# Sums of weight quarters in a seven-product matmul: from accumulating DMAs to VectorE and GpSimd

## The chip, the cores and the metric

The kernel runs on one core of a Trainium2 chip. The metric is device time in microseconds. The kernel before took 545.22, 550.09 and 551.16 us in three runs, a median of 550.09 us. The profiled execution that all rows below come from took 547.97 us, of which the recorded span is 546.2 us.

A core has five engines with instruction streams of their own, each worked off in order: TensorE (PE in the profile, with its weight loads as PEld), VectorE (DVE), ScalarE (ACT), GpSimd (POOL) and SyncE (SP, which here only issues DMAs). Data wait in on-chip memory (SBUF); TensorE writes its results to PSUM; 16 DMA engines move data from and to DRAM. A semaphore tells one engine that another, or a DMA, is done.

## The reference

Two residual layers over x of 512 rows and 1024 columns, in float32:

```
layer 0: h = rms_norm(x);  y = h @ W_in          # one projection, its columns are:
         [FoX q,k,v | forget logits | MoBA q,k,v | gate]
         FoX attention (8 heads, decay bias)  ||  MoBA attention (8 heads, rotary, top-3 blocks)
         x = x + (concat(heads) * silu(gate)) @ W_out
layer 1: h = rms_norm(x);  y = h @ W_in1          # GLU value | GLU gate | gate
         GLU -> causal depthwise conv (31 taps) -> layer norm -> swish -> * silu(gate)
         x = x + y @ W_out1
```

The change is in layer 0's input projection.

## The kernel before

**Products.** A float32 matmul is done as three matmuls: both sides are split into a high part of type float32r and the rest, and hi·hi, hi·lo and lo·hi are added in PSUM. `parts_of` makes such a split: an ACT copy for the high part (L412), then a DVE subtraction for the rest (L413). A split result is called an operand here.

**Seven products.** Ten of the column chunks of 256 columns of layer 0's projection are taken in five pairs (`PAIRS`, n = 0 to 4). The two chunks of a pair, 1024 x 512 values, are cut into four quarters: "11" and "12" are the upper 512 rows of the first and the second chunk, "21" and "22" the lower ones. A quarter lies in SBUF as 128 x 1024 float32, 512 KB. A Strassen-like scheme multiplies a pair with 7 products in place of 8. `product` (L608) is 24 matmuls of 128x256. The left sides (sums of quarters of h) are made once, ahead; the right sides are, with b for the quarters of the pair:

| product | 1 | 7 | 2 | 5 | 6 | 3 | 4 |
|---|---|---|---|---|---|---|---|
| right side | b11 | b12+b22 | b21 | b11+b12 | b11+b12+b22 | b22 | b11+b12+b21+b22 |

Each right side is one operand: one L412 and one L413, 35 in all. This text writes (n,m) for product m of pair n and op(n,m) for its operand. The list `PRODS` orders them as 7, 2, 5, 6 of pair n, then 1 of pair n+1, then 3 and 4 of pair n. `make_to` makes operands two products ahead (`AHEAD`), into three buffers.

**Staging.** Two tiles of SBUF (`stage`, tag "wst") hold four quarters, that is one pair. A quarter of the next pair is fetched by SP into the place of a quarter that is done with. The first four pairs use L559; the last pair's columns are split, so its fetches are the lines L561, L563 and L564.

**Sums in the kernel before.** They are made by DMA: GpSimd issues a transfer from DRAM with `accum_op=add`, which adds a quarter to one that is staged. Four stand in each pair: b22 onto "12" when "12" has been fetched; then "12" onto "11" once op(n,1) is made; "11" onto "12" once op(n,7) is made; "21" onto "12" once op(n,6) is made. All sums but that of op(n,5) end in the place "12", which op(n,7), op(n,6) and op(n,4) are read from. A DMA of this kind waits on the DVE subtraction that read its place last.

**What runs beside it.** The products are interleaved with attention work (`advance`, `PACE`): q and k are scaled and split (L757 and L758, L766 to L768), logits are formed (L777, L779), masked with their row maximum (L789, DVE), exponentiated (L790, ACT), transposed (L793, L803) and multiplied by v (L874). After each product ACT and DVE combine results (L627, L642 to L646: the running sums of the scheme), and rows are normalized (L483 to L501 on ACT, DVE and GpSimd, the rotary steps L505 to L511 on GpSimd). The framework's scheduler fixes each engine's order when the program is built. Layer 1 comes after, from about 300 us; there GpSimd and DVE share the convolution (L1042, L1052).

Of the kernel before, what the change touches and what calls it, by code (L numbers as in the profile page):

```python
# [14 lines left out]
ALU = mybir.AluOpType  # L15
# [14 lines left out]
WC = 256  # L30
# [63 lines left out]
PAIRS = ((2, 5), (3, 4), (7, 8), (10, 11), (9, 6))  # L94
# [4 lines left out]
def tile_kernel(ctx: ExitStack, tc: tile.TileContext, x, xt, w, small0, small1, l1_norm, out):  # L99
# [15 lines left out]
    V, A, G, T, SY = nc.vector, nc.scalar, nc.gpsimd, nc.tensor, nc.sync  # L115
# [52 lines left out]
    def w_cols(i, k, c, m):  # L168

        off, n = wsrc[i]  # L170
        return bass.AP(tensor=w.tensor, offset=w.offset + off + k * n + c,
                       ap=[[KC * n, P], [n, KC // 2 if m != NH else KC], [1, m]])

    def w_ap(off, n, k, m):
        return bass.AP(tensor=w.tensor, offset=w.offset + off + k * n,
                       ap=[[KC * n, P], [1, m * n]])
# [58 lines left out]
    HK = KC // 2  # L235
    HT = S // 2

    def operand(x):

        x = x.rearrange("p (j k n) -> p j k n", j=2, k=HK)  # L240
        return x[:, 0], x[:, 1]
# [34 lines left out]
    wsrc = []  # L276
# [112 lines left out]
    for t in range(NT):  # L389
        ts = slice(t * P, (t + 1) * P)  # L390
        for h in range(2):
# [3 lines left out]
                            op=ALU.mult)  # L395
# [14 lines left out]
    def parts_of(x, dst, eng=V):  # L410
        hi, lo = dst
        A.activation(hi, x, AF.Copy)  # L412
        eng.tensor_tensor(lo, x, hi.bitcast(F32), op=ALU.subtract)  # L413
# [100 lines left out]
    def qk_chunk(i, key, rope_i):  # L514
# [12 lines left out]
        if i:  # L527
# [8 lines left out]

    place = {"11": 0, "12": 1, "21": 2, "22": 3}

    NEXT = {"11": "21", "12": "11", "21": "22", "22": "12"}
    places = []  # L540


    OPERANDS = {1: ("11", "12"), 7: ("12", "11"), 2: ("21", None), 5: ("11", None),
                6: ("12", "21"), 3: ("22", None), 4: ("12", None)}

    PRODS = [(n + a, m) for n in range(-1, len(PAIRS)) for a, m in
             ((0, 7), (0, 2), (0, 5), (0, 6), (1, 1), (0, 3), (0, 4)) if 0 <= n + a < len(PAIRS)]
# [2 lines left out]
    def quarter(n, q):  # L550
        j = places[n][q]
        return stage[j // 2][:, j % 2 * HK * WC:(j % 2 + 1) * HK * WC].rearrange(
            "p (k n) -> p k n", k=HK)

    def from_b(queue, n, q, d, **kw):

        i, k = PAIRS[n][int(q[1]) - 1], (int(q[0]) - 1) * HK
        if n < FPAIR:
            queue.dma_start(d.rearrange("p k n -> p (k n)"), w_ap(*wsrc[i], k, HK), **kw)  # L559
        elif q[1] == "1":  # L560
            queue.dma_start(d, w_cols(i, k, 0, WC), **kw)  # L561
        else:
            queue.dma_start(d[:, :, 4:], w_cols(i, k, 0, WC - 4), **kw)  # L563
            queue.dma_start(d[:, :, :4], w_cols(PAIRS[n][0], k, WC, 4), **kw)  # L564

    def fetch_quarter(n, q):
        if n >= len(PAIRS):
            return
        if n == len(places):
            places.append({x: places[-1][y] for x, y in NEXT.items()} if n else  # L570
                          {"11": 0, "12": 1, "21": 2, "22": 3})
        from_b(SY, n, q, quarter(n, q))
        if q == "12":
            from_b(G, n, "22", quarter(n, q), accum_op=ALU.add)

    def fetch_first():
        for _ in range(2):
            stage.append(main.tile([P, KC * WPAD], F32, tag="wst", name="stage", bufs=2))
        for q in ("11", "12", "21", "22"):
            fetch_quarter(0, q)  # L580
# [4 lines left out]
    def make_to(g):  # L585

        while made[0] <= min(g, len(PRODS) - 1):
            n, m = PRODS[made[0]]
            q, more = OPERANDS[m]
            tag = slots[made[0] % 3]  # L590
            made[0] += 1
            ops[n, m] = operand(main.tile([P, KC * WPAD], F32R, tag=tag, name="op",
                                          bufs=2 if tag == "whi" else 1)[:, :2 * HK * WC])
            parts_of(quarter(n, q), ops[n, m])
            if more:
                from_b(G, n, more, quarter(n, q), accum_op=ALU.add)
            for x, y in NEXT.items():
                if y == q and m in (2, 5, 3, 4):
                    fetch_quarter(n + 1, x)

    def product(po, a, b, new):
# [9 lines left out]
    def pairs_of_chunks(jobs):  # L611
# [7 lines left out]
        for g, (n, m) in enumerate(PRODS):  # L619
            job = jobs[n]  # L620
            make_to(g + AHEAD)
            b = ops.pop((n, m))
            if m == 1:
# [277 lines left out]
    def dense():  # L901
        with tc.issue_after(hpart.ins):
            split(1)
        fetch_first()
        sums()
        yield from qk_chunk(0, ("moba", "q", 0), 0)
        make_to(1)
        yield from qk_chunk(1, ("moba", "k", 0), 1)
        last_sum()
        for j, _ in enumerate(pairs_of_chunks((Values("moba"), QK("moba", 1, True), QK("fox", 0, False),  # L910
                                               QK("fox", 1, False), Values("fox")))):
            if j == len(PRODS) - 3:
                fetch(12)
                fetch(13)
            yield
        split(12)
        spread_rinv()
        for c in range(4):
            fetch(14 + c)
            split(13 + c)  # L920
            yield from gate_chunk(12 + c, c)
# [29 lines left out]
    for k in KORD:  # L951
# [3 lines left out]
        eng = G if k in GLO else V  # L955
# [200 lines left out]
    for c in range(1, 4):  # L1156
        i = 20 + 2 * c
# [91 lines left out]
    n = max(len(v6), len(v7))  # L1249
# [38 lines left out]
    with tc.manual_schedule(engines=engs):  # L1288
# [19 lines left out]
        for p in range(4):  # L1308
            k = 2 * p
# [153 lines left out]
```

## Time and profile before

| | |
|---|---|
| three runs | 545.22, 550.09, 551.16 us, median 550.09 |
| profiled execution | 547.97 us, span 546.2 us |
| TensorE busy | 507.4 us, 93% of the span |
| weight loads (beside PE) | 453.3 us, 83% |
| VectorE busy | 406.5 us, 74% |
| ScalarE busy | 344.8 us, 63% |
| GpSimd busy | 241.0 us, 44% |
| DMA by GpSimd's queue (q0) | 9216 packets, 37.75 MB, 32.4% of 16 engines' span |
| DMA by the hardware queues (q1) | 18616 packets, 51.08 MB, 26.4% |

Busy shares say how much an engine has to do, not whether it is waited for: that is read from the chain of waits (the work that ended last, followed back from the end) and from the timelines. The granted clock of TensorE (PEclk) is given as a share of 2.4 GHz; 0.5 in a stretch means 1.2 GHz.

### The profile page before, as it was taken

Reading aid. Unit: us, or ns where it says so; the run is one execution under the profiler, and the core shown is the slowest. Engines: PE = TensorE matmul, PEld = TensorE weight load, DVE = VectorE, ACT = ScalarE, POOL = GpSimd, SP = SyncE. Lnnn points to the kernel's source line nnn. Section 1 sums busy time; section 2 is a strip of 40 time slices with the busy share of each in tenths; the row PEclk is TensorE's granted clock in tenths of the full one; section 3 lists DMA queues with packets and bytes.
Section 4 is the critical chain, followed back from the end, with each engine's and each line's share of the span. In section 5 each row is a group of like instructions: output and inputs, shape, how many; then the busy total and the mean of one; then the engine's idle time right before and its main releaser. Section 6 shows DMA issues by size and latency. Waiting matters only on the chain.

```text
span 546.2 us, 9635 instructions
## 1 busy us (share of the span) xinstructions
PE 507.4 (93%) x3574; PEld 453.3 (83%) x3574; DVE 406.5 (74%) x819; ACT 344.8 (63%) x655; POOL 241.0 (44%) x269
## 2 busy tenths in 40 slices
PE   8999898987799879999999999999999999869997
PEld 4998797787687757887868999999999988649997
DVE  7997478675777657777769434999999999668841
ACT  4964598635677749656648553788869675568230
POOL 4269010193702511232312011587999885867300
PEclk9999799998889979999999999999999999979999
DMA  8787675167821533532123786469989989962111
GB/s 293 265 190 158 166 156 135 63 130 189 152 51 56 101 113 132 177 117 94 56 84 130 305 183 224 134 164 209 311 244 230 308 242 307 256 197 87 59 45 44
DMA packets 28023, 89.54 MB, mean 164 GB/s; under 512 B 5636, under 2 KB 13120, under 8 KB 21576
## 3 DMA queue, kind: packets, MB, share of 16 engines
q0 software_dynamic: 9216, 37.75, 32.4%
q1 hardware_dynamic: 18616, 51.08, 26.4%
q8 instruction: 28, 0.46, 0.3%
q10 hardware_dynamic: 144, 0.09, 0.1%
q14 instruction: 19, 0.16, 0.1%
HBM read 60.56 MB, written 2.14 MB: 115 GB/s over the span
## 4 chain that ended last, share of the span: by engine, by line
PE 57%; DMA 13%; ACT 12%; DVE 9%; issue 4%; POOL 3%; SPq 1%; POOLq 0%; ACTq 0%; DVEq 0%
PE m L458 8%; PE m L467 7%; PE m L468 7%; PE m L469 7%; PE m L608 5%; DMA stage<-in_w_dram 5%; PE st L458 4%; PE st L874 3%; DMA wst<-in_w_dram 3%; PE o L608 3%; ACT op L412 2%; DMA wx<-wst 2%; POOL pacc L1052 2%; PE tp L793 2%; PE o L458 2%
## 5 line engine op out<-in xcount | busy, mean ns | idle before, releaser
L1052 POOL TENSOR_TENSOR pacc<-pacc,tm 128x256 f32<-128x256 f32 (+1 forms) x125 | 120.7, 982 | 16.2 <-ACT tm L1051 10.1
L1042 DVE SCALAR_TENSOR_TENSOR s<-u,parts,s 128x256 f32<-128x256 f32 (+1 forms) x211 | 108.2, 572 | 0.5
L1051 ACT ACTIVATE tm<-u,parts 128x256 f32<-128x256 f32 (+1 forms) x125 | 66.2, 571 | 12.5 <-POOL pacc L1052 11.9
L413 DVE TENSOR_TENSOR op<-stage,op 128x1024 fp32r<-128x1024 f32 x35 | 43.9, 1256 | 23.0 <-ACT op L412 22.8
L412 ACT ACTIVATE op<-stage 128x1024 fp32r<-128x1024 f32 x35 | 36.8, 1054 | 25.6 <-DMA stage<-in_w_dram 15.1
L608 PE MATMUL m<-op,s 128*128 128x256 f32 x360 | 49.9, 292 | 0.8 <-DVE op L413 0.4
L790 ACT ACTIVATE p<-p,nm 128x128 f32<-128x128 f32 (+3 forms) x64 | 35.7, 558 | 21.8 <-DVE nm L789 19.9
L785 POOL TENSOR_TENSOR late<-late,mask 128x128 f32<-128x128 f32 x32 | 18.1, 569 | 70.5 <-DVE nm L789 54.0
L608 PEld LDWEIGHTS m<-op,s 128*128 128x128 f32 x360 | 46.7, 198 | 2.1 <-DVE op L413 0.8
L498 POOL TENSOR_TENSOR rq<-vq,mhalf 128x16 f32<-128x16 f32 x8 | 23.4, 2932 | 55.3 <-DVE vq L496 36.3
L559 POOL DMA_DIRECT2D stage<-in_w_dram x16 | 17.2, 1115 | 40.9 <-DVE op L413 34.4
L467 PE MATMUL m<-nhi,wx 128*128 128x256 f32 (+1 forms) x104 | 33.3, 320 | 0.0
L608 PE MATMUL m<-op,hhi 128*128 128x256 f32 x160 | 31.0, 289 | 1.7 <-ACT o L627 1.7
L469 PE MATMUL m<-nhi,wx 128*128 128x256 f32 (+1 forms) x104 | 32.4, 311 | 0.0
L468 PE MATMUL m<-nlo,wx 128*128 128x256 f32 (+1 forms) x104 | 32.3, 311 | 0.0
L468 PE MATMUL m<-nlo,whi 128*128 128x256 f32 (+1 forms) x104 | 31.9, 308 | 0.0
L203 ACT ACTIVATE whi<-wst 128x512 fp32r<-128x512 f32 (+2 forms) x37 | 27.5, 800 | 7.0 <-DMA wst<-in_w_dram 3.9
L467 PE MATMUL m<-nhi,whi 128*128 128x256 f32 (+1 forms) x104 | 31.8, 307 | 0.0
L469 PE MATMUL m<-nhi,wl 128*128 128x256 f32 (+1 forms) x104 | 31.8, 306 | 0.0
L793 PE MATMUL tp<-identf,p 128*128 128x128 f32 x160 | 28.2, 280 | 1.6 <-DVE pt L803 0.8
L777 PE MATMUL s<-k,q 128*128 128x256 f32 (+2 forms) x64 | 23.4, 374 | 5.8 <-ACT k L767 5.3
L608 PEld LDWEIGHTS m<-op,hhi 128*128 128x128 f32 x160 | 25.2, 191 | 2.4 <-ACT o L627 2.3
(331 smaller groups left out, 1649.4 us busy)
## 6 DMA issues: line engine op xcount, KB each, us to landing
wst<-in_w_dram SPq DMA_DIRECT2D x24, 1024.0 KB, 5.5
wx<-wst POOLq DMA_DIRECT2D x13, 1024.0 KB, 7.2
stage<-in_w_dram SPq DMA_DIRECT2D x18, 512.0 KB, 4.4
stage<-in_w_dram POOLq DMA_DIRECT2D x18, 512.0 KB, 6.7
wl<-wst POOLq DMA_DIRECT2D x8, 1024.0 KB, 7.9
whi<-wst POOLq DMA_DIRECT2D x3, 1024.0 KB, 4.9
xs<-in_x_dram SPq DMA_DIRECT2D x4, 512.0 KB, 6.0
late<-cdram SPq DMA_DIRECT2D x8, 256.0 KB, 3.1
```

Source lines behind the costliest of these rows:

```text
L412: A.activation(hi, x, AF.Copy)
L413: eng.tensor_tensor(lo, x, hi.bitcast(F32), op=ALU.subtract)
L458: T.matmul(po, a[:, k, ts], b[:, k, :n], start=first and i == 0, stop=last and i == len(prods) - 1)
L467: T.matmul(po, whi[:, k, cs], a, start=k == 0, stop=False)
L468: T.matmul(po, whi[:, k, cs], b, start=False, stop=False)
L469: T.matmul(po, wlo[:, k, cs], a, start=False, stop=k == KC - 1)
L608: T.matmul(po[:, cs], x[:, k, ts], y[:, k], start=new and j == 0 and k == 0 and m == 0, stop=k == HK - 1 and m == 2, skip_group_check=True)
L790: A.activation(p[:, :w], p[:, :w], AF.Exp, bias=nm, scale=-1.0, accum_out=sm[:, h, t:t + 1])
L793: T.transpose(tp[:, j * P:(j + 1) * P], p[:, j * P:(j + 1) * P], identf)
L1042: V.scalar_tensor_tensor(acc[:, o], v, w, first[0][:, :n] if i == 1 else acc[:, o], op0=ALU.mult, op1=ALU.add)
L1051: A.activation(tm[:, :n], v, AF.Copy, scale=w)
L1052: G.tensor_tensor(pacc[:, o], pacc[:, o], tm[:, :n], op=ALU.add)
```

## The change

The sums are no longer made by DMA. `make_to` now makes them in place, in SBUF, from the staged quarters, and all in the place "11" but one:

- before op(n,7) is split: "11" += "12", then "12" += "22", both on DVE (new line L591)
- behind op(n,5): "11" += "22", on DVE (new line L598)
- behind op(n,6): "11" += "21", on GpSimd (L598 too)

So there are 15 additions of 128 x 1024 on DVE, 5 on GpSimd, and no accumulating DMA. op(n,6) and op(n,4) are read from "11". The places and times of SP's fetches change with `NEXT` and `LAST`: "11" of pair n+1 goes to the place of "12" once op(n,7) is made (before: to that of "21" once op(n,2) is made); "12" goes to the place of "21" once op(n,6) is made and the GpSimd addition has read "21" (before: to that of "11" once op(n,5) is made); "22" follows op(n,3), "21" follows op(n,4). The number of SP fetches stays: 20 quarters. Lines from about L603 on stand 2 further down after the change (L643 becomes L645, L789 becomes L791).

```diff
-    NEXT = {"11": "21", "12": "11", "21": "22", "22": "12"}
+    NEXT = {"11": "12", "12": "21", "22": "22", "21": "11"}
+
+    LAST = {"12": 7, "21": 6, "22": 3, "11": 4}
     places = []
...
-    OPERANDS = {1: ("11", "12"), 7: ("12", "11"), 2: ("21", None), 5: ("11", None),
-                6: ("12", "21"), 3: ("22", None), 4: ("12", None)}
+    OPERANDS = {1: ("11", (), ()), 7: ("12", (("11", "12", V), ("12", "22", V)), ()), 2: ("21", (), ()),
+                5: ("11", (), (("11", "22", V),)), 6: ("11", (), (("11", "21", G),)),
+                3: ("22", (), ()), 4: ("11", (), ())}
...
-        from_b(SY, n, q, quarter(n, q))
-        if q == "12":
-            from_b(G, n, "22", quarter(n, q), accum_op=ALU.add)
+        from_b(n, q, quarter(n, q))
...
-            q, more = OPERANDS[m]
+            q, before, behind = OPERANDS[m]
+            for x, y, eng in before:
+                eng.tensor_tensor(quarter(n, x), quarter(n, x), quarter(n, y), op=ALU.add)
...
             parts_of(quarter(n, q), ops[n, m])
-            if more:
-                from_b(G, n, more, quarter(n, q), accum_op=ALU.add)
+            for x, y, eng in behind:
+                eng.tensor_tensor(quarter(n, x), quarter(n, x), quarter(n, y), op=ALU.add)
             for x, y in NEXT.items():
-                if y == q and m in (2, 5, 3, 4):
+                if m == LAST[y]:
                     fetch_quarter(n + 1, x)
```

The scheduler places the engines' instructions anew between about 26 and 210 us of the kernel before; behind that the orders of all engines are the same. Two places on DVE follow. The first is where pair 0 ends and pair 1 begins. Before, the four subtractions L413 of the piece are those of op(0,6), op(1,1), op(0,3) and op(0,4), in that order; L643 to L646 are the combining steps of product (0,6):

```order
L413 TENSOR_TENSOR op<-stage,op 128x1024
L719 COPY ct<-st 8x512
L413 TENSOR_TENSOR op<-stage,op 128x1024
L501 TENSOR_TENSOR qk<-qk,rq 128x1024
L413 TENSOR_TENSOR op<-stage,op 128x1024
L643 TENSOR_TENSOR m_722<-m_722,u_807 128x512
L645 TENSOR_TENSOR o<-o,v_76 128x512
L413 TENSOR_TENSOR op<-stage,op 128x1024
L646 TENSOR_TENSOR v_76<-m_722,v_76 128x2x256
```

After, op(0,6) stands five rows further up, and the piece begins with the subtraction of op(0,3); the next L413 is that of op(0,4), the last two are those of op(1,7) and op(1,2); L645 to L648 are the combining steps:

```order
L413 TENSOR_TENSOR op<-stage,op 128x1024
L591 TENSOR_TENSOR stage<-stage 128x1024
L645 TENSOR_TENSOR m_720<-m_720,u_805 128x512
L647 TENSOR_TENSOR o<-o,v_76 128x512
L413 TENSOR_TENSOR op<-stage,op 128x1024
L591 TENSOR_TENSOR stage<-stage 128x1024
L721 COPY ct<-st 8x512
L648 TENSOR_TENSOR v_76<-m_720,v_76 128x2x256
L413 TENSOR_TENSOR op<-stage,op 128x1024 x2
```

The two additions L591 for op(1,7) now stand one ahead of and one behind the subtraction of op(0,4). The second place is in pair 1, ahead of the first logits tiles. Before, the row x2 is op(1,2) and op(1,5), the next L413 is op(2,1), the last one op(1,6), behind three logits tiles (`kl` is the rest of a split k, `s` a tile of logits, `nm` its row maximum):

```order
L413 TENSOR_TENSOR op<-stage,op 128x1024 x2
L768 SCALAR_TENSOR_TENSOR kl_82<-st,gsc,k_80 64x512
L413 TENSOR_TENSOR op<-stage,op 128x1024
L768 SCALAR_TENSOR_TENSOR kl_83<-st,gsc,k_81 64x512
L789 ISA p,nm<-s,mask 128x128
L789 ISA nm 128x1
L789 ISA p,nm<-s,mask 128x128
L789 ISA nm 128x1
L789 ISA p,nm<-s,mask 128x256
L789 ISA nm 128x1
L413 TENSOR_TENSOR op<-stage,op 128x1024
```

After, the row x2 is op(2,1) and op(1,6), the next L413 is op(1,3), and the same logits tiles come behind both:

```order
L413 TENSOR_TENSOR op<-stage,op 128x1024 x2
L486 TENSOR_REDUCE ssq<-m_828 128x8
L770 SCALAR_TENSOR_TENSOR kl_82<-st,gsc,k_80 64x512
L413 TENSOR_TENSOR op<-stage,op 128x1024
L770 SCALAR_TENSOR_TENSOR kl_83<-st,gsc,k_81 64x512
L591 TENSOR_TENSOR stage<-stage 128x1024
L791 ISA p,nm<-s,mask 128x128
L791 ISA nm 128x1
L791 ISA p,nm<-s,mask 128x128
L791 ISA nm 128x1
L591 TENSOR_TENSOR stage<-stage 128x1024
L791 ISA p,nm<-s,mask 128x256
```

The subtractions of op(1,6) and op(1,3) moved ahead of the logits tiles, and the two additions for op(2,7) stand among these tiles: the first, "11" += "12" of pair 2, four rows behind the subtraction of op(1,6) and ahead of the first tile.

## Rows read from the trace of the kernel before

**Rows 1.** The page: engines' busy us, then the chain that ended last by engine

```profile
PE 507.4 (93%) x3574; PEld 453.3 (83%) x3574; DVE 406.5 (74%) x819; ACT 344.8 (63%) x655; POOL 241.0 (44%) x269
...
PE 57%; DMA 13%; ACT 12%; DVE 9%; issue 4%; POOL 3%; SPq 1%; POOLq 0%; ACTq 0%; DVEq 0%
```

**Rows 2.** Busy time by engine in stretches (start:end length, busy, PEclk, DMA share, GB/s)

```profile
33.00:217.00 184.00, 161.88 (x1160) 142.80 (x1158) 127.24 (x240) 120.42 (x234) 65.56 (x64) 0.94 0.55 124
55.00:64.00 9.00, 6.30 (x30) 5.87 (x29) 4.55 (x5) 4.26 (x7) 0.88 (x1) 0.64 0.61 166
120.00:131.00 11.00, 5.96 (x37) 5.76 (x36) 4.36 (x6) 3.15 (x5) 4.80 (x9) 0.84 0.86 212
400.00:450.00 50.00, 49.77 (x358) 46.55 (x357) 49.97 (x85) 36.66 (x49) 45.39 (x40) 1.00 0.91 261
```

**Rows 3.** The chain of waits, 0 to 260 us (start, length, what)

```profile
47.39 8.71 DMA stage<-in_w_dram
56.17 1.06 ACT op L412
57.26 1.24 DVE op L413
58.54 5.28 PE o L608 x23
...
114.94 9.46 DMA stage<-in_w_dram
124.48 1.06 ACT op L412
126.04 4.30 PE m L608 x24
...
177.16 6.48 DMA stage<-in_w_dram
183.72 1.06 ACT op L412
```

**Rows 4.** Waits by engine, 33 to 217 us (total us, times, longest)

```profile
POOL stage L559 <- DVE op L413: 34.4, 5, 10.7
DVE op L413 <- ACT op L412: 22.8, 14, 4.1
```

**Rows 5.** TensorE's timeline at the waits (start, length; idle before and releaser in brackets)

```profile
57.28 0.42 PE L608 MATMUL o<-op,hhi 128*128 128x256 f32 x1 [1.86 <-ACT op L412]
58.54 0.58 PE L608 MATMUL o<-op,hhi 128*128 128x256 f32 x1 [0.84 <-DVE op L413]
...
125.59 0.45 PE L608 MATMUL o<-op,hhi 128*128 128x256 f32 x1 [5.04 <-ACT op L412]
125.84 4.50 PE L608 MATMUL m<-op,s 128*128 128x256 f32 x24
...
133.37 3.00 PE L608 MATMUL m<-op,s 128*128 128x256 f32 x24
...
184.83 0.39 PE L608 MATMUL o<-op,s 128*128 128x256 f32 x1 [0.84 <-ACT op L412]
```

**Rows 6.** Groups by line and shape: DVE in 33 to 217 us, GpSimd over the span

```profile
L413 DVE TENSOR_TENSOR op<-stage,op 128x1024 fp32r<-128x1024 f32 x33 | 41.4, 1258 | 23.0 <-ACT op L412 22.8
L501 DVE TENSOR_TENSOR qk<-qk,rq 128x1024 f32<-128x1024 f32 x8 | 9.7, 1220 | 1.1 <-POOL rq L499 1.0
L768 DVE SCALAR_TENSOR_TENSOR kl<-st,gsc,k 64x512 fp32r<-64x512 f32 x12 | 8.9, 739 | 3.2 <-ACT k L767 3.1
L486 DVE TENSOR_REDUCE ssq<-m 128x8 f32<-128x512 f32 x6 | 4.0, 673 | 3.0 <-ACT m L485 3.0
L643 DVE TENSOR_TENSOR m<-m,u 128x512 f32<-128x512 f32 x5 | 3.5, 694 | 0.5 <-ACT u L642 0.3 <-PE m L608 0.2
...
L1052 POOL TENSOR_TENSOR pacc<-pacc,tm 128x512 f32<-128x512 f32 x40 | 54.2, 1389 | 1.7 <-ACT pacc L1048 0.5
```

**Rows 7.** DMA issues, 33 to 217 us (count, KB each, median us to landing)

```profile
stage<-in_w_dram POOLq DMA_DIRECT2D x16, 512.0 KB, 6.6
stage<-in_w_dram SPq DMA_DIRECT2D x13, 512.0 KB, 3.8
```

**Rows 8.** DVE's timeline: the subtractions around the first wait

```profile
45.47 1.62 DVE L413 TENSOR_TENSOR op<-stage,op 128x1024 fp32r<-128x1024 f32 x1 [1.73 <-ACT op L412]
...
57.26 1.23 DVE L413 TENSOR_TENSOR op<-stage,op 128x1024 fp32r<-128x1024 f32 x1 [3.19 <-ACT op L412]
```

**Rows 9.** GpSimd's timeline: one step beside a DVE subtraction, and without one

```profile
39.61 1.75 POOL L505 TENSOR_TENSOR tab<-qk,ropeA 128x256 f32<-128x256 f32 x1
...
121.81 0.72 POOL L505 TENSOR_TENSOR tab<-qk,ropeA 128x256 f32<-128x256 f32 x1
```

More of the change, by code (lines that the diff above doesn't have):

```diff
@@ L553, in quarter, with from_b @@
             "p (k n) -> p k n", k=HK)
-    def from_b(queue, n, q, d, **kw):
+    def from_b(n, q, d):
         i, k = PAIRS[n][int(q[1]) - 1], (int(q[0]) - 1) * HK
         if n < FPAIR:
-            queue.dma_start(d.rearrange("p k n -> p (k n)"), w_ap(*wsrc[i], k, HK), **kw)
+            SY.dma_start(d.rearrange("p k n -> p (k n)"), w_ap(*wsrc[i], k, HK))
         elif q[1] == "1":
-            queue.dma_start(d, w_cols(i, k, 0, WC), **kw)
+            SY.dma_start(d, w_cols(i, k, 0, WC))
         else:
-            queue.dma_start(d[:, :, 4:], w_cols(i, k, 0, WC - 4), **kw)
-            queue.dma_start(d[:, :, :4], w_cols(PAIRS[n][0], k, WC, 4), **kw)
+            SY.dma_start(d[:, :, 4:], w_cols(i, k, 0, WC - 4))
+            SY.dma_start(d[:, :, :4], w_cols(PAIRS[n][0], k, WC, 4))
     def fetch_quarter(n, q):
```

## The prediction

> **What bounds the kernel now.** I read the page's busy shares first, then its chain by engine, then the table of stretches, the chain of waits in order of time, and last TensorE's timeline at each wait that the chain shows. TensorE is busy for 507.4 of 546.2 us and is 57% of the chain; DMA is 13%, ScalarE 12%, DVE 9% [rows 1]. So TensorE sets the time, and what can be gained is the time in which it stands still or runs at half its clock. The changed part lies between 33 and 217 us: there TensorE works 161.88 of 184.00 us at a mean granted clock of 0.94, DVE 127.24 us (69%), GpSimd 65.56 us (36%) [rows 2]. So DVE has 57 us of room in this stretch and GpSimd 118 us.
>
> The chain enters that stretch's accumulating DMAs three times: 8.71 us from 47.39, 9.46 us from 114.94, 6.48 us from 177.16, each followed by the ScalarE copy of a split [rows 3]. They are those that op(0,4), op(2,4) and op(4,6) wait for. On TensorE they cost much less than their 24.65 us, because work is ahead of it: it stood idle 1.86 us and, after one matmul, 0.84 us more at the first, 5.04 us at the second, 0.84 us at the third [rows 5]. Behind the first two its granted clock falls to 1.2 GHz for a while, which makes the mean 0.64 in 55 to 64 us and 0.84 in 120 to 131 us [rows 2]: 23 matmuls in 5.28 us [rows 3] and 24 in 4.50 us, against 24 in 3.00 us a little later [rows 5]. So the first wait costs 2.7 + (5.28 - 2.9) = 5.1 us, the second 5.04 + 1.50 = 6.5 us, the third 0.8 us: 12.4 us in all is what the accumulating DMAs take on TensorE.
>
> **The change part by part.** The sum is made against the profiled execution's 547.97 us, which lies 2.1 us under the median of 550.09; I add 2.1 at the end.
>
> *The second wait, -6.5 us.* op(2,4) needs "21" added to a place that op(2,6) was read from. Before, a transfer has to be issued and to land (9.46 us); after, it is one GpSimd addition. GpSimd has no addition of 128 x 1024 in this trace; the nearest is L1052, 1389 ns for 128 x 512 while DVE works beside it [rows 6], so an estimate for twice the size is 2.6 to 2.8 us; I use 2.6. That is 6.9 us less, more than the 5.04 us that TensorE stood, so the wait goes, and its slow clock with it: -6.5 us. Bounds: 0 if something else is late there, -6.5 at most. What is late next is the split itself (ScalarE 1.06 us and DVE 1.24 us) [rows 3]. The third wait goes by the same reason: -0.8 us (0 to -0.8).
>
> *The first wait, 0.* Before, it takes 11.4 us from the end of op(0,6)'s subtraction (45.47 + 1.62) to the end of op(0,4)'s (57.26 + 1.23) [rows 8]. After, op(0,4) itself needs GpSimd's addition only (2.6 us). But in DVE's new order an L591, "11" += "12" of pair 1, stands ahead of op(0,4)'s subtraction, and its "12" is fetched by SP only when the GpSimd addition has read "21". So: 2.6 addition + 3.8 SP fetch [rows 7] + 1.22 addition on DVE (by L501, two float32 inputs and the same shape [rows 6]) + two steps of 0.69 (L643's kind) + 1.23 subtraction = 10.2 us against 11.4. On the other hand the three DVE additions of pair 0 (two before op(0,7), one behind op(0,5)) now stand ahead of op(0,6): up to 3.7 us later, in place of three accumulating DMAs that were partly waited for there. Net between -1.2 and +2.5; I take 0, since both sides rest on rows of nearly the same size.
>
> *A new wait in pair 1, +2.5 us.* The first L591 for op(2,7) stands four rows behind op(1,6)'s subtraction on DVE: L486 0.67, L768's kind 0.74, L413 1.26, L768's kind 0.74, 3.4 us [rows 6]. What it needs takes 2.6 (GpSimd addition) + 3.8 (fetch) = 6.4 us. So DVE stands up to 3.0 us there, and queued behind it are the first logits tiles, that ScalarE's exponentials and TensorE's transposes wait for. If that comes through to TensorE it may also lower the clock, as the first wait did: up to 3.0 + 3.4 (the clock's price doubled for a product and the tiles behind it) = 6.4 us. If TensorE has products in hand, it is 0. I take 2.5, the wait nearly whole without the clock, since the waits of this stretch reach TensorE at one third to one half of their length (5.04 of 9.46, 2.7 of 8.71 [rows 3, 5]) but this one also holds back the attention tiles. At the next two boundaries 13 and 19 rows stand between, so nothing there.
>
> *Fifteen additions on DVE, +2.2 us.* 15 x 1.22 = 18.3 us [rows 6]. In 33 to 217 us DVE stands 57 us idle, 22.8 us of it in 14 waits of L413 for ScalarE [rows 2, 4], so they fit; what reaches the end is their share of DVE work on the chain: 9% of 546.2 = 49 us out of 406.5 busy [rows 1], 12%, hence 2.2 us. Bounds: 0 (all in DVE's gaps) and 18.3 (all on the path).
>
> *Five additions on GpSimd, twenty issues less, 0.* 5 x 2.6 = 13 us are hidden by GpSimd's idle time in the stretch; where the addition is waited for it is counted above. If GpSimd is held up by its rotary work there, one addition is late by some 2 us. The accumulating issues that waited in GpSimd's queue, 34.4 us in five long waits [rows 4], are gone, and nothing on the chain was behind them. The transfers fall by 16 x 512 KB and more [rows 7]; the fetches of SP could land sooner than 3.8 us, which I count at 0.
>
> Sum: -6.5 - 0.8 + 0 + 2.5 + 2.2 + 0 = -2.6. 547.97 - 2.6 + 2.1 = **547.5 us**.
>
> *A rule that speaks against this.* GpSimd's and DVE's work can slow each other: GpSimd's L505 took 1.75 us beside a DVE subtraction and 0.72 us without one [rows 9]. But from 400 to 450 us DVE is busy for 49.97 us and GpSimd for 45.39 us of the same 50, both with additions and multiply-adds from SBUF, L1052 at 1389 ns each [rows 2, 6]; two engines that shut each other out could not both be busy so long. The Trainium skill, "SBUF — State Buffer", section "Who interferes with whom", says that a DVE instruction with two SBUF inputs contends with a GpSimd instruction that reads SBUF, and that the shared pair of ports is held for the whole instruction. The first of these two readings agrees with that rule, the second does not, unless blocked time counts as busy. By it every addition here would shut out the other engine: that is rival C.
>
> **Rivals.**
>
> *A, all three waits go and nothing comes.* If SP's fetches land sooner without the accumulating traffic and pair 0's additions fall in DVE's gaps, the first wait goes too: -5.1 - 6.5 - 0.8 + 2.2 = -10.2, **540 us**. For it: the sum on op(0,4) is a 2.6 us addition, and DVE has 57 us of room. Against: L591 ahead of op(0,4), and the order rows in pair 1.
>
> *B, slower: DVE waits in order for a fetch.* Each next pair's "12" now comes only after op(n,6), GpSimd's addition and a fetch (6.4 us at least), where before it was fetched after op(n,5). If the scheduler's places for L591 are too early at the boundaries from pair 1 to 2, 2 to 3 and 3 to 4, DVE stands 3.0 us at each with tiles behind it, and the clock's price of 1.5 comes on top: 3 x 4.5 - 7.3 + 2.2 = +8.4, **558 us**. It decides, against the waits saved (7.3 less 2.2), from 1.7 us on TensorE at each of the three. For it: the first boundary's order rows; against: 13 and 19 rows at the other two.
>
> *C, GpSimd and DVE shut each other out.* With L505's ratio of 1.75 to 0.72, 2.4, the GpSimd addition takes 6.2 us in place of 2.6. At the first wait this is 3.6 us more, of which 1.2 is covered: +2.4; in pair 1 another +3.6: -2.6 + 6.0 = +3.4, **553.5 us**. For it: rows 9. Against: the stretch from 400 to 450 us.
>
> That the change doesn't do what it says is no rival: no accumulating issue is left, and the additions stand in the order.
>
> **Chances.** The forecast 0.42 (543 to 552), A 0.30, B 0.18, C 0.10. The median of 550.09 has runs from 545.22 to 551.16, so about 1% (5.5 us) is what can be told from no change: below 544.6 is faster, above 555.6 slower. Faster: A's 0.27 and 0.10 of the forecast's, 0.37. Slower: 0.16 of B and 0.03 of C, 0.19. The same: 0.44. The range from 538 to 558 leaves out A's lower end (0.08) and B's upper half (0.09).
>
> **What would show it.** Right: no wait of L412 for a DMA at (0,4), (2,4) and (4,6) in the chain, the stretch at 120 us at full clock, and additions of 1.2 us on DVE and 2.6 to 2.8 us on GpSimd. Wrong: L591 or L598 in the chain with more than 5 us, or DVE idle ahead of an L591 for a stage fetch by over 3 us more than once (B); GpSimd additions of over 4 us (C); the half clock behind the first wait gone (A). Were the DVE additions themselves on the path, DVE's share of the chain would rise from 9% to 12% or more.

## The result, and the profile after

The changed kernel took a median of 551.89 us over 20 runs (549.13 to 555.68), the kernel before 547.23 us over 20 runs (544.07 to 554.64). The ratio is 1.0085, interval 1.006 to 1.0109: 4.7 us slower. I had forecast 2.6 us faster. The time lies inside the range, the sign is wrong. The profiled execution took 551.01 us, span 549.2, so 3.0 us more than the profiled one of before.

The page of the kernel after, its busy engines and its chain by engine; they answer to [rows 1]:

```profile
PE 509.4 (93%) x3574; PEld 455.8 (83%) x3574; DVE 429.6 (78%) x834; ACT 346.0 (63%) x655; POOL 236.8 (43%) x252
...
PE 56%; DVE 11%; POOL 11%; DMA 10%; ACT 7%; issue 4%; SPq 0%; POOLq 0%; DVEq 0%; ACTq 0%
```

DVE has 23 us more work, more than the 18.3 us of the 15 additions (the timelines of DVE below say where more comes from). What is new is GpSimd: it works less than before and yet goes from 3% to 11% of the chain. The stretch of the change, from the table of stretches (the same columns as [rows 2]), runs 2 us longer at about the same clock; the transfers' share fell from 0.55 to 0.22:

```profile
33.00:219.00 186.00, 163.65 (x1152) 144.87 (x1152) 148.36 (x253) 119.69 (x230) 61.03 (x48) 0.93 0.22 69
```

The chain of waits shows what took the place of the accumulating DMAs of [rows 3]:

```profile
49.40 3.35 POOL stage L598
52.77 3.69 DMA stage<-in_w_dram
56.48 1.23 DVE stage L591
...
106.60 5.78 POOL rq L498 x2
112.73 3.34 POOL stage L598
116.07 1.69 POOL tab L505
...
122.99 1.59 POOL qk L511
124.63 0.67 PE st L752 x4
...
148.43 2.36 POOL stage L598
151.23 3.35 DMA stage<-in_w_dram
```

First the GpSimd addition, then SP's fetch that waits for it, then DVE's L591 that waits for the fetch: that is the path I had worked out for the first wait. The second place, 106 to 125 us, I had not: there the addition stands in GpSimd's queue behind two L498 and ahead of the rotary steps, and TensorE waits for the last of these. TensorE's timeline (answers to [rows 5]) shows the first wait as long as before, 2.02 + 0.68 us against 1.86 + 0.84, the 5 us wait gone, and the new one on L511:

```profile
59.06 0.35 PE L610 MATMUL o<-op,hhi 128*128 128x256 f32 x1 [2.02 <-DVE o L647]
60.09 0.58 PE L610 MATMUL o<-op,hhi 128*128 128x256 f32 x1 [0.68 <-DVE op L413]
...
124.63 0.66 PE L752 MATMUL st<-identf,qk 128*128 128x128 f32 x4 [1.79 <-POOL qk L511]
```

And DVE's timeline holds the rows that decide the case, beside those of GpSimd's addition. First GpSimd, then DVE:

```profile
49.36 3.38 POOL L598 TENSOR_TENSOR stage<-stage 128x1024 f32<-128x1024 f32 x1
...
112.69 3.38 POOL L598 TENSOR_TENSOR stage<-stage 128x1024 f32<-128x1024 f32 x1
...
148.39 2.38 POOL L598 TENSOR_TENSOR stage<-stage 128x1024 f32<-128x1024 f32 x1
```

```profile
48.73 1.75 DVE L501 TENSOR_TENSOR qk<-qk,rq 128x1024 f32<-128x1024 f32 x1
50.41 2.39 DVE L710 TENSOR_TENSOR ft<-ft 128x32 f32<-128x32 f32 x1
...
112.59 4.57 DVE L501 TENSOR_TENSOR qk<-qk,rq 128x1024 f32<-128x1024 f32 x2 [0.52 <-POOL rq L499]
...
148.46 3.40 DVE L501 TENSOR_TENSOR qk<-qk,rq 128x1024 f32<-128x1024 f32 x1 [0.52 <-POOL rq L499]
```

L501 takes 1.22 us alone [rows 6]. At 148.46 it starts 0.07 us after the addition and takes 3.40, nearly 1.22 + 2.38 - 0.07: it does nothing until the addition is over. At 112.59 it is DVE that starts first: the addition takes 3.38 in place of 2.38, 1.0 us longer, about what the first L501 has left, and then the second L501 waits for it, so that two take 4.57 in place of 2.4. L710, 128 x 32 values, took 2.39. All of them read two operands from SBUF. The waiting counts as busy, on either engine. Over the stretch the eight L501 take 14.5 us, against 9.7 before [rows 6].

### The profile page after: what moved, and what is told of

Read it like the earlier page. It is cut to its first block, busy times and chain, and to the rows that moved or that the text cites. A ratio compares the mean times of both kernels' runs of the same rounds, so it can differ in the third digit from the quotient of the medians.

```text
span 549.2 us, 9586 instructions
## 1 busy us (share of the span) xinstructions
PE 509.4 (93%) x3574; PEld 455.8 (83%) x3574; DVE 429.6 (78%) x834; ACT 346.0 (63%) x655; POOL 236.8 (43%) x252
## 4 chain that ended last, share of the span: by engine, by line
PE 56%; DVE 11%; POOL 11%; DMA 10%; ACT 7%; issue 4%; SPq 0%; POOLq 0%; DVEq 0%; ACTq 0%
PE m L458 8%; DMA wst<-in_w_dram 7%; PE m L467 7%; PE m L468 7%; PE m L469 6%; PE m L610 5%; PE st L458 4%; POOL pacc L1054 3%; PE o L610 3%; PE st L876 3%; POOL rq L498 3%; DVE op L413 2%; DMA stage<-in_w_dram 2%; PE tp L795 2%; PE o L458 2%
## 5 line engine op out<-in xcount | busy, mean ns | idle before, releaser
L498 POOL TENSOR_TENSOR rq<-vq,mhalf 128x16 f32<-128x16 f32 x8 | 24.4, 3063 | 79.3 <-DVE vq L496 79.3
L610 PE MATMUL m<-op,s 128*128 128x256 f32 x360 | 51.6, 297 | 0.6 <-ACT qk L633 0.2
L413 DVE TENSOR_TENSOR op<-stage,op 128x1024 fp32r<-128x1024 f32 x35 | 43.5, 1243 | 9.6 <-ACT op L412 9.5
L610 PEld LDWEIGHTS m<-op,s 128*128 128x128 f32 x360 | 47.8, 202 | 1.9 <-ACT qk L633 0.7
L795 PEld LDWEIGHTS tp<-identf,p 128*128 128x128 f32 x160 | 20.2, 145 | 8.8 <-ACT p L792 4.9
```

What stands on the lines that cost most here:

```text
L498: G.tensor_tensor(r, v, mhalf[:, :16].rearrange("p (t h) -> p t h", t=NT), op=ALU.pow)
L610: T.matmul(po[:, cs], x[:, k, ts], y[:, k], start=new and j == 0 and k == 0 and m == 0, stop=k == HK - 1 and m == 2, skip_group_check=True)
L795: T.transpose(tp[:, j * P:(j + 1) * P], p[:, j * P:(j + 1) * P], identf)
```

## The experiments

Most experiments keep the order of every engine, all waits and all issues of the kernel that they start from: an instruction is altered only after the scheduler has placed everything. That matters here, since the scheduler places the stretch anew at each edit of the source. The cut, for e1 to e3 (all, or those of one engine, of the 20 additions):

```diff
     with _tile.TileContext(nc, schedule_with_timeline_sim=True) as tc:
         tile_kernel(tc, *args)
+    short = {i.name for n, m, pool, i in ADDS if pool}
...
+                bb.instructions = [cut(i) if i.name in short else i for i in bb.instructions]
```

`ADDS` holds the additions, `pool` tells GpSimd's (e1; `not pool` in e2, all in e3), and `cut` makes their operands 128 partitions by 8 columns.

Theories: **V**, the additions on DVE are the price. **G**, the GpSimd additions are. **O**, the new order and the later fetches are. Within G: **L**, GpSimd and DVE shut each other out while both read from SBUF (rival C); **Q**, the addition's mere length on the way to the next fetch and in GpSimd's queue.

**e1, GpSimd's additions cut.**

> The changed kernel with every instruction in the same place and the same waits, but each of the 5 GpSimd additions covers 8 columns in place of 1024 (so the sums of quarters are left out there). After itself is 1.0085 of before. Theory G (GpSimd's in-order queue: in the trace of after an addition takes 2.4 to 3.4 us, stands behind two L498 of 2.9 us, and holds up the rotary steps behind it for 18 us in a row around 107 to 125 us): 1.002 or less, 3.5 us or more gained. Theory V (the 15 additions on DVE are the price): 1.006 to 1.0085, at most 1.5 us gained. Theory O (the new order of the attention work and the later fetches are the price): 1.005 or more.

0.9943 (0.9912 to 0.9974): 1.4% of 547 us, 7.8 us less than after. G holds; beyond the first wait and that of pair 1 I had counted these additions at nothing. TensorE's wait on L511 is gone in the trace of e1.

**e2, DVE's additions cut.**

> The changed kernel with the same order and waits, but each of the 15 DVE additions covers 8 columns in place of 1024 (so the sums of quarters are left out there): about 17 us less work on DVE. Theory V: 0.995 or less, 7 us or more gained, nearly half of the 17. My prediction's 12% share: 2.2 us gained, 1.0045. Theory G: 1.006 or more, at most 1.5 us gained. Theory O: 1.004 or more.

0.9968 (0.994 to 0.9996): 6.4 us less than after; the interval is 1.5 us to either side. V holds too, just short of its 7 us, with 0.43 us for each addition of 1.22. That is 35% of their time on the path, not the 12% that I took from DVE's share of the chain.

**e3, both.**

> Both shortenings together: all 20 additions cover 8 columns (the sums are left out), order, waits and fetches as in the changed kernel. This is what the new order and the new fetches cost or bring with sums that are nearly free. Theory O: still 1.003 or more. Theories V and G: below 0.990, since then the waits for accumulating DMAs that the change took away (12.4 us by my count) show.

0.9872 (0.9837 to 0.9908), 11.7 us less than after; the two prices nearly add (14.2). This is below 0.990, as V and G had it, and O's 1.003 is out. But it stays above what e4, the next run, shows for the kernel before without its accumulating DMAs, so part of what the change took away was given back elsewhere.

**e4, the accumulating DMAs of before cut.** `cut` on the 22 accumulating transfers of the kernel before.

> The kernel before with the same order, issues and waits, but each accumulating DMA moves 8 columns (4 in the four smallest) in place of up to 1024, so the sums are left out. This prices what the accumulating DMAs cost before. By my count of TensorE's stalls and slow clock (5.1 + 6.5 + 0.8): 12.4 us, 0.977. If DMA waits of that kind are mostly covered by other waits (the stall goes, but TensorE then waits for attention work instead): 0.990 to 1.000.

0.9791 (0.9752 to 0.983): 11.4 us less than before, 2.1 to either side. The count of TensorE's stalls and slow clock, 12.4 us, agrees with it as a whole; the three waits were not priced one by one. The chain of e4 has DMA at 6% in place of 13%:

```profile
PE 62%; ACT 9%; POOL 8%; DVE 7%; DMA 6%; issue 5%; SPq 0%; POOLq 0%; DVEq 0%; ACTq 0%
```

**e8 and e11, the fetches cut as well.** SP's fetches of pairs 1 to 4 get the same cut: in e8 on top of e3, in e11 on top of e4.

> e3 with SP's fetches of pairs 1 to 4 cut to 8 columns as well, order and waits as in the changed kernel (fetches and sums of quarters are left out). e3 was at 0.9872, e4 at 0.9791, so 4.4 us lie in the new order and the later fetches. If the fetches behind the additions are that: 0.981 or less. If it is the order of the attention work: 0.985 or more.

> The kernel before with the same order and waits, accumulating DMAs and SP's fetches of pairs 1 to 4 all cut to 8 columns (sums and fetches of quarters left out). Against e8 (0.9782), the same of the changed kernel, it shows what the two orders differ by when neither waits for sums or fetches. If the changed order is no worse: 0.976 to 0.980. If it is worse by the 4.4 us between e3 and e4: 0.971 or less.

e8 0.9782 (0.9745 to 0.9818), e11 0.9809 (0.978 to 0.9839). In the changed kernel, with its sums nearly free, the fetches cost 0.9872 - 0.9782, 4.9 us; in the kernel before nothing that can be told (0.9791 to 0.9809). e8 is below the 0.981 expected if the fetches are the price; e11 lies a thousandth above the 0.980 expected if the orders are alike. With neither sums nor fetches the two orders are alike within the intervals, some 2 us to either side of each. So of theory O the fetches hold, and the new order of the attention work falls. Which of the fetches cost the 4.9 us was not tried one by one; the chain of after has that of "12", which comes only behind op(n,6) and its addition, twice (52.77 and 151.23 us).

**e7, the GpSimd additions in eight pieces.** A piece is the same instruction on 128 columns; the first has the waits, the last the signal.

> The changed kernel with the same order and waits, but each GpSimd addition is cut into 8 instructions of 128 columns, one right behind the other; the computation is whole. Theory L: DVE gets in between the pieces, so L501 beside an addition takes 1.9 us or less in place of 3.40, and of the 7.8 us 3 or more are gained: 1.003 or less. Theory Q: the addition gets no shorter (8 pieces take 2.4 us or more): 1.0085 or more.

1.0225 (1.0183 to 1.0266), 7.7 us slower than after. By the letter this is Q's side (pieces of over 2.4 us, 1.0085 or more), but neither theory had a time so long, and L501 did get short as L had it. The timelines of GpSimd and of DVE say why:

```profile
115.49 6.37 POOL L598 TENSOR_TENSOR stage<-stage 128x128 f32<-128x128 f32 x8
...
152.04 4.37 POOL L598 TENSOR_TENSOR stage<-stage 128x128 f32<-128x128 f32 x8
...
195.95 3.36 POOL L598 TENSOR_TENSOR stage<-stage 128x128 f32<-128x128 f32 x8
```

```profile
115.39 2.63 DVE L501 TENSOR_TENSOR qk<-qk,rq 128x1024 f32<-128x1024 f32 x2 [0.71 <-POOL rq L499]
```

DVE is free: two L501 take 2.63 us, not 4.57. Now GpSimd is late: 4.37 and 6.37 us for what took 2.38 and 3.38. About 1.0 us of this is the cutting itself, since at 195.95 us, where DVE runs nothing with two inputs from SBUF, the pieces still take 3.36 us against 2.38 for the whole. The rest is waiting between the pieces: the waiting has changed sides, and on GpSimd's side it lies on the way to the next fetch. DVE's ten L591 say so, in after and in e7 (the last columns are DVE's idle time ahead of them):

```profile
L591 DVE TENSOR_TENSOR stage<-stage 128x1024 f32<-128x1024 f32 x10 | 12.2, 1225 | 4.5 <-DMA stage<-in_w_dram 4.5
...
L591 DVE TENSOR_TENSOR stage<-stage 128x1024 f32<-128x1024 f32 x10 | 12.2, 1220 | 13.6 <-DMA stage<-in_w_dram 13.6
```

So the shutting out is real, but e7 could not price it: it removed one cost and raised others.

**e9, the same with nothing read.** Each addition is replaced, in place, by 8 GpSimd instructions that write counters into the same columns.

> The changed kernel with the same order and waits, but each GpSimd addition is replaced by 8 GpSimd instructions that write counters into the same 1024 columns and read nothing from SBUF (so these sums are left out); together they should take about as long as the addition, 2 to 2.6 us. After is 1.0085, e1 (no length, no reading) 0.9943. Theory L (the price is that DVE is shut out while GpSimd reads): DVE's L501 beside them takes 1.3 us or less, and the time falls to 0.998 or less. Theory Q (the price is the addition's length on the way to the next fetch and in GpSimd's queue): L501 may fall as well, but the time stays at 1.004 or more. About half and half: 1.001.

0.9964 (0.994 to 0.9989), 6.6 us less than after. GpSimd's and DVE's timelines:

```profile
109.33 1.53 POOL L598 IOTA stage<- 128x128 int32 x8
143.23 1.54 POOL L598 IOTA stage<- 128x128 int32 x8
```

```profile
109.23 2.36 DVE L501 TENSOR_TENSOR qk<-qk,rq 128x1024 f32<-128x1024 f32 x2
...
143.31 1.23 DVE L501 TENSOR_TENSOR qk<-qk,rq 128x1024 f32<-128x1024 f32 x1 [0.52 <-POOL rq L499]
```

GpSimd works beside L501 as before, reads nothing, and one L501 takes 1.23 us, two 2.36. The eight L501 of the stretch and L710 take 10.1 and 0.2 us, against 14.5 and 2.4 in after: DVE gets 6.6 us back. TensorE's wait on L511 is gone too.

The writing is shorter than I meant, 1.54 us against 2.38, so not all of the 6.6 us of time is the shutting out. What the missing 0.84 us in each of the five cost can only be estimated. From e1 to e9 the five together get 4.7 us longer (3.0 to 7.7) and that cost 1.2 us; at this rate the missing 4.2 us cost 1.0. From after to e7 they get 9.9 us longer (13.9 to 23.8) and that cost at least 7.7 us, since DVE gained at the same time; at this rate they cost 3.3. So of the 7.8 us of e1 some 3 to 6 go to L, as an estimate, and the rest to Q. The intervals, 1.4 us to either side for e9 and 1.7 for e1, come on top.

**e5, all additions on DVE.**

```diff
-                5: ("11", (), (("11", "22", V),)), 6: ("11", (), (("11", "21", G),)),
+                5: ("11", (), (("11", "22", V),)), 6: ("11", (), (("11", "21", V),)),
```

> The changed kernel with the fifth addition of each pair ("11" += "21") on DVE too; the scheduler places the instructions anew. From e1 and e2: the 5 GpSimd additions cost 7.8 us, a DVE addition 6.4/15 = 0.43 us. Theory L (a GpSimd addition shuts DVE's instructions with two inputs from SBUF out for its whole length, and that is its price): 7.8 - 5 x 0.43 = 5.7 us gained on after, 0.998, give or take the 4 us that a new order can make. Theory Q (it is the addition's length on the way to the next fetch): the same sign, less, since a DVE addition stands in a fuller queue: 1.002 to 1.006.

0.9927 (0.9899 to 0.9954): 543.18 us, 8.6 us less than after and 4.0 less than before. The expectation of L was 0.998; the other 3 us are within what it allowed for the new order, and are not explained further. Q had expected less gain, 1.002 to 1.006, but with a new order, and an addition that is also shorter on DVE (1.2 us against 2.4), e5 does not part L from Q.

**e6, only the sum that was waited for.**

```diff
-    NEXT = {"11": "12", "12": "21", "22": "22", "21": "11"}
+    NEXT = {"11": "11", "12": "21", "21": "22", "22": "12"}
...
-    LAST = {"12": 7, "21": 6, "22": 3, "11": 4}
+    LAST = {"11": 5, "21": 6, "22": 3, "12": 4}
...
+    OPERANDS = {1: ("11", (), (("11", "12", G),)), 7: ("12", (), (("12", "11", G),)), 2: ("21", (), ()),
+                5: ("11", (), ()), 6: ("12", (), (("12", "21", V),)),
+                3: ("22", (), ()), 4: ("12", (), ())}
```

Here, and in e10, G stands for an accumulating DMA that GpSimd issues.

> Only the sum that the chain of before waited for moves from a DMA to DVE: "12" += "21" behind op(n,6), 5 additions; the sums b22 onto "12", "12" onto "11" and "11" onto "12" stay accumulating DMAs. "21" now stays until that addition, so "11" of the next pair goes to the place of "11" behind op(n,5), and "12" to that of "21" behind op(n,6). From e4: up to 11.6 us of waits gone, 5 x 0.43 = 2.1 us of DVE added: 0.983, give or take 4 us for the order. Should the later "12" with its accumulation (3.8 + 6.6 us) be the next wait: 0.995 to 1.005.

0.9986 (0.996 to 1.0013): no change. The chain of e6:

```profile
55.74 10.85 DMA stage<-in_w_dram
...
88.01 11.12 DMA stage<-in_w_dram
...
124.18 9.24 DMA stage<-in_w_dram
```

The fetch of "12" now starts later and still has its accumulation behind it, and this pair of transfers is the new wait, at each change of pair. A stall was moved, as the last sentence of the expectation had it.

**e10, three additions on DVE, one early DMA.** As e5, but "11" += "12" is an accumulating DMA behind op(n,1):

```diff
-    OPERANDS = {1: ("11", (), ()), 7: ("12", (("11", "12", V), ("12", "22", V)), ()), 2: ("21", (), ()),
+    OPERANDS = {1: ("11", (), (("11", "12", G),)), 7: ("12", (("12", "22", V),), ()), 2: ("21", (), ()),
```

> e5 with "11" += "12" made by an accumulating DMA again, issued behind op(n,1) as in before, where three to five products lie between it and its first reader op(n,5); the other three additions of a pair stay on DVE, 15 in all. By e2's 0.43 us for a DVE addition 5 x 0.43 = 2.1 us less than e5: 0.989, give or take 4 us for the new order. If an accumulating DMA is waited for there too (6.6 us, and its transfers slow SP's fetches): 0.994 or more.

0.9905 (0.988 to 0.9931): 540.83 us, 5.2 us less than before and the fastest that computes everything, near the 0.989 expected; against e5 the difference is inside the intervals. Its chain has TensorE at 65%:

```profile
PE 65%; DVE 9%; ACT 9%; DMA 8%; POOL 5%; issue 3%; SPq 0%; POOLq 0%; ACTq 0%; DVEq 0%
```

## Why the prediction was wrong

The runs give a sum of their own, each term the difference of two ratios times 547 us, from before over e4, e11, e8 and e3 to after: the accumulating DMAs -11.4, the fetches of before +1.0 (that is what e11 lies above e4) and the order -1.5 (neither of them clear of zero), the fetches of after +4.9, the additions on both engines +11.7; together +4.7.

**Waits of the accumulating DMAs: right.** 12.4 us counted, 11.4 measured. What I credited to the change was 7.3, since I let the first wait stand; that too was right, 2.70 us then and 2.70 now on TensorE. To compare the forecast with the runs' sum, the first wait's 5.1 us have to be taken apart: the old cause is in the -11.4, and the new one (addition, fetch and L591) is in the +4.9 and the +11.7. The forecast's additions, fetches and new waits are then 5.1 + 2.5 + 2.2 = 9.8 us, and the runs say 16.6. These 6.8 us are nearly the whole miss of 7.3.

**A new wait in pair 1, +2.5: right in kind.** DVE's timeline of after has it, 2.13 us against up to 3.0 expected:

```profile
82.82 1.23 DVE L591 TENSOR_TENSOR stage<-stage 128x1024 f32<-128x1024 f32 x1 [2.13 <-DMA stage<-in_w_dram]
```

The 4.9 us of e8 are the price of all fetches, the first wait's share among them. What this wait alone cost TensorE was not measured.

**Fifteen additions on DVE, +2.2: too small.** e2 measured 6.4. The step that failed is the 12%: DVE's share of the chain of before, taken as the price of work that is added to it. That the share was taken over the whole span is the lesser part of it: from 33 to 217 us the pieces of DVE on the chain of before add up to some 21 of its 127 us, 17%, which would have given 3.1 us. The measured share was 35%. The chain of after has 6 of the 15 additions whole in it, from 36.17 to 157.13 us, 6.9 us:

```profile
36.17 1.13 DVE stage L591
56.48 1.23 DVE stage L591
100.22 1.13 DVE stage L598
129.24 1.14 DVE stage L591
138.59 1.13 DVE stage L598
157.13 1.14 DVE stage L591
```

So idle time of DVE covered about two thirds of the 18.3 us, not seven eighths. Why it covered no more, no run shows.

**Five additions on GpSimd, 0: the step whose mechanism was wrong.** e1 measured 7.8 us. Part of this is not this item's, since the forecast had 2.6 us of addition in the first wait and again in that of pair 1, and e1 shortens both; how much, was not separated. But "hidden by GpSimd's idle time" looked at GpSimd alone. An instruction that shuts another engine out is not hidden by its own engine's idle time: DVE was held for 6.6 us (after against e9). And at 112.73 us the addition stood in GpSimd's own queue ahead of rotary steps that TensorE waited for. The mechanism was in the prediction as rival C with a chance of 0.10, and was put aside with the sentence that two engines that shut each other out could not both be busy for 50 us. That reading fails twice. Blocked time counts as busy, as L501's 3.40 us show. And the stretch from 400 to 450 us was the wrong witness: DVE's taps there (L1042) add into an accumulator that the code takes from a bank of PSUM, so they have one input in SBUF. The kernel has two taps of the same size whose second input (`first`) is in SBUF, and these rows of the trace of before, groups of DVE from 400 to 450 us, had the answer:

```profile
L1042 DVE SCALAR_TENSOR_TENSOR s<-u,parts,s 128x512 f32<-128x512 f32 x53 | 36.3, 746 | 0.0
L1042 DVE SCALAR_TENSOR_TENSOR s<-u,parts,first 128x512 f32<-128x512 f32 x2 | 3.8, 1888 | 0.0
```

Beside the same additions of GpSimd the form with one SBUF input takes 746 ns and the form with two 1888 ns, the mean of two. The Trainium skill, "SBUF — State Buffer", section "Who interferes with whom", says that an instruction of DVE with two inputs in SBUF contends with a GpSimd instruction that reads SBUF, and not with one that only writes it. The same page of the Trainium skill, section "SBUF: two separate sides", says that whichever of the two starts first holds the shared pair for the whole instruction. The traces of after and e9 agree with the three statements: L501 takes 3.40 us beside an addition and 1.23 beside the writing, and at 112.59 us, where DVE starts first, it is the addition that takes 3.38 in place of 2.38.

Either of the two mis-sized terms alone would have turned the sign: -2.6 + 4.2 for DVE's additions, and -2.6 with more than a third of e1's 7.8.

Rival C's 553.5 us came nearest to the measured time, though by another road: I had multiplied the addition's length by L505's ratio of 2.4, to 6.2 us, and it took 2.4 to 3.4. What grew was DVE's side, so C's sign, additions of over 4 us, did not show. A sign against the forecast did, L598 in the chain with 9 us. DVE's share of the chain rose from 9% to 11%, just short of the 12% named. Rival B's condition, DVE standing 3.0 us for a fetch at each of three boundaries, is not what came: DVE's idle time ahead of all ten L591 is 4.5 us. That the time fell within the range is luck and a wide range: the forecast stood on a median of before of 550.09 us from three runs, and twenty runs have 547.23, so the time came 2.9 us nearer to it than the change did.

**Not settled.** How the 7.8 us divide between L and Q is open, from 3 to 6 us for L by the estimate at e9; writing as long as the additions would have told more. Why e5 gained 3 us more than its terms give was not tried; its order differs from that of after.

## What to carry to other kernels

A wait that the chain shows is worth what the stall and the slow clock behind it cost on the bounding engine, and that can be read off well (12.4 against 11.4 us). What takes its place has to be priced as carefully: an engine's share of the chain of before, 12% of its work or 17% in the stretch, was no price for work added to that engine, which cost 35%. Before moving work to an idle GpSimd, ask what DVE does meanwhile and where its inputs lie: here an addition of 2.4 us on GpSimd cost three to four times as much as one of 1.2 us on DVE (7.8/5 = 1.6 against 0.43 us, the queue behind it included). To test one cause in a kernel whose scheduler reorders at each edit, change the instructions after they are placed.

## What was not expected of the hardware

Cutting a GpSimd instruction into pieces to let DVE through made the whole slower by 7.7 us: in 8 pieces the addition took 3.4 to 6.4 us in place of 2.4 to 3.4. About 1 us of it is the cutting itself, and the rest waiting: the median piece took 0.46 us, the longest 1.45. And GpSimd's add of 128 x 1024 takes 2.38 us when DVE leaves it alone, near the 2.6 estimated from L1052.
